# Adding transfers for the square sums, plain products three tiles behind, and the token scale spread inside the third plain tile

## The chip, the cores and the metric

The kernel runs on one core of a Trainium2 chip. Its time is the device time of one execution in microseconds (us); of several runs the median counts. The engines are TensorE (PE, matmuls), VectorE (DVE), ScalarE (ACT), GpSimd (POOL) and SyncE (SP, which here issues the DMA transfers).

## The reference, cut to what matters

The model is a trunk of two layers over 1024 frames of width 1024. Layer 0 mixes with stick-breaking attention and a pooling branch, layer 1 with gated linear attention. After the mixer each layer adds a feed-forward part with a depthwise convolution, and its input is normalised:

```python
def rms_norm(x, gain):
    xf = x.astype(jnp.float32)
    y = xf * lax.rsqrt(jnp.mean(xf * xf, axis=-1, keepdims=True) + NORM_EPS)
    return (y * gain.astype(jnp.float32)).astype(x.dtype)
...
def conv_ffn(h, w_up, conv_w, conv_b, w_down):
    u = h @ w_up
...
    a, g = jnp.split(conv, 2, axis=-1)
    return (jax.nn.silu(a) * g) @ w_down
...
x = x + conv_ffn(rms_norm(x, ffn_norm[layer]), ffn_w_up[layer], ...)
```

The case is about the entry into `h @ w_up`: the end of the mixer's output projection, the sum of squares of x over its 1024 channels, and the first columns of the up-projection.

## The kernel before, in words

The activations lie transposed: eight tiles x[0] to x[7] of 128 channels (partitions) by 1024 frames, in float32. A product in near-float32 precision is made of three matmuls in a faster format (`mm3`, lines 137, 139, 141): each operand is split into a high and a low part, and high x high, high x low and low x high are summed in PSUM. PSUM has eight banks of 128 x 512; in this stage the tags lin, z, t and d name two banks each, taken in turn (`bank`).

`ffn` is called once in each layer. Its entry, which this text calls entry A in layer 0 and entry B in layer 1, goes like this. `add_tiles` (from line 809) makes the last two row blocks of the mixer's output projection for one tile of x, 12 matmuls, first for frames 0 to 511 into a bank of t, then for frames 512 to 1023 into a bank of d; after each half DVE adds the bank to x (line 819). `NormBlocks.add` (line 293) then spills x to memory through SP (line 295), makes the tile's two blocks (line 289 on ACT the high part, line 290 on DVE the low part, with the gain already in), squares x on ACT (lines 306, 309) and adds the square to the accumulator nacc on DVE (line 310). Tiles come in the order 0, 4, 1, 5, 2, 6, 3, 7 (`ORDER`). Two tiles behind, `first_tile` (line 976) lets the tile enter two ordinary ("plain") products of the up-projection, 12 matmuls: column tile 0 into the banks lin with the weights s12h and s12l, and its gate into the banks z with s34h and s34l.

After the eight tiles `stats` (line 258) sums nacc over partitions by matmuls with ones (line 261), takes the root on ACT (264) and the reciprocal on DVE (266), and puts it on a diagonal dg (line 268; the tile is called ndg in A and nsq in B). `plain(1)` makes a third plain column tile, 48 matmuls in eight steps of six, into banks of t and d. Then `spread` (line 273) multiplies dg by ones into a bank of d and one of t (line 275), which gives the reciprocal root for each frame on all partitions, and ACT copies it to rstd_bc (276). DVE multiplies the three finished column tiles by rstd_bc to u (line 1008), and `plain(FT + 1)`, the fourth plain tile, takes the banks lin and z again. From then on the up-projection goes by pairs in a Strassen-like scheme (`Pair`, matmuls on line 885), whose operands `rsums` and `rblock` (lines 905 to 908 and 864, 865) prepare from x during the entry. The pair's first evacuations are tm on ACT (926, 933, 941) and u on DVE (937, 942, 948, 952).

Three things set the order of the work. PE runs in the order in which the code is written. The instructions of DVE, ACT, POOL and SP are ordered by the framework's scheduler when the kernel is built, and each engine then works through its queue in that order and waits at its head. Large buffers come from pools: x, nacc, the squares, T4 and u share eleven slots of 128 x 1024 (`slot`), the blocks share sixteen (`hpool`), and a new tile waits for the old one in its slot.

Of the kernel before, what the change touches and what calls it, by code (L numbers as in the profile page):

```python
# [13 lines left out]
AF = mybir.ActivationFunctionType  # L14
ALU = mybir.AluOpType
# [4 lines left out]
KT = D // P  # L20
# [36 lines left out]
def trunk_kernel(  # L57
# [23 lines left out]
    V, S, G, PE = nc.vector, nc.scalar, nc.gpsimd, nc.tensor  # L81
# [21 lines left out]
    def bank(tag):  # L103
        return psum.tile([P, 512], F32, tag=f"bank{next(turns[tag])}", name=tag)
# [4 lines left out]
    ORDER = [0, 4, 1, 5, 2, 6, 3, 7]  # L109


    def load_split(src, pool=None, tags=("whi", "wlo", "wraw"), eng=None, nb=2, raw=None, parts=None):
        n = src.shape[1]
        pool = pool or wpool
        if raw is None:
            raw = (pool if len(tags) > 2 else wpool).tile([P, n], F32, tag=tags[2] if len(tags) > 2 else "wraw",
                                                      name="wraw", bufs=2 if "draw" in tags else 1)
        hi = pool.tile([P, n], R32, tag=tags[0], name="whi", bufs=nb)
        lo = pool.tile([P, n], R32, tag=tags[1], name="wlo", bufs=nb)

        def part(cs):
            nc.sync.dma_start(raw[:, cs], src[:, cs])
            S.copy(hi[:, cs], raw[:, cs])  # L123
            (eng or V).tensor_tensor(lo[:, cs], raw[:, cs], hi[:, cs].bitcast(F32), op=ALU.subtract)  # L124

        if parts is not None:
            parts.extend(lambda cs=cs: part(cs) for cs in HALVES)
        else:
            part(slice(0, n))
        return hi, lo  # L130

    def mm3(out, w, a, first, last):

        (wh, wl), (ah, al) = w, a
        n = len(out)
        for i in range(n):
            PE.matmul(out[i], wh, ah[i], start=first, stop=False)  # L137
        for i in range(n):
            PE.matmul(out[i], wh, al[i], start=False, stop=False)  # L139
        for i in range(n):  # L140
            PE.matmul(out[i], wl, ah[i], start=False, stop=last)  # L141
# [11 lines left out]
    class Filler:  # L153
# [3 lines left out]
        def add(self, *gens):  # L157
            self.gens += gens
# [119 lines left out]
    class NormBlocks(Norm):  # L278
# [14 lines left out]
        def add(self, m, x):  # L293
            xs[m] = dram.tile([P, T], F32, tag=f"xs{self.layer}_{m}", name="xs")
            nc.sync.dma_start(xs[m], x)
            g = pcol(self.col + m)
            if m < KT // 2:
                self.b11.append(self.block(x[:, 0:512], g))
                self.b12.append(self.block(x[:, 512:T], g))
            else:  # L300
                self.b21.append(self.block(x[:, 0:512], g))
                self.b22.append(self.block(x[:, 512:T], g))
            self.n += 1
            if self.n == 1:
                self.acc = self.acc_tile()
                S.activation(self.acc, x, AF.Square)
            else:
                sq = self.sq_tile()
                S.activation(sq, x, AF.Square)
                V.tensor_tensor(self.acc, self.acc, sq, op=ALU.add)  # L310
            if m < KT // 2:
                S.activation(x, x, AF.Copy, scale=g)

# [22 lines left out]
    def pcol(c):  # L336
        return prm[:, c:c + 1]
# [244 lines left out]
    x = [None] * KT  # L582
# [227 lines left out]
    def add_tiles(ws, acts, tags, ms):  # L810
        n = len(ws)
        pss = {m: [bank(next(tags)), bank(next(tags))] for m in ms}
        for i, cs in enumerate(HALVES):
            for m in ms:
                sl = slice(m * P, (m + 1) * P)
                for k in range(n):
                    mm3([pss[m][i]], (ws[k][0][:, sl], ws[k][1][:, sl]),
                        ([acts[k][0][:, cs]], [acts[k][1][:, cs]]), k == 0, k == n - 1)
                V.tensor_tensor(x[m][:, cs], x[m][:, cs], pss[m][i], op=ALU.add)  # L819
# [7 lines left out]
    def ffn(layer, nm, after, ow, mixt, onward=None):  # L827
# [10 lines left out]
        def raw_a(i):  # L838
            raw = wpool.tile([P, T], F32, tag="wraw", name="wraw", bufs=1)
            nc.sync.dma_start(raw, wup[layer, i])  # L840
            hi = wpool.tile([P, T], R32, tag="whi", name="whi")
            lo = wpool.tile([P, T], R32, tag="wlo", name="wlo")
            S.copy(hi, raw)
            V.tensor_sub(lo, raw, hi.bitcast(F32))
            return raw, hi, lo
# [30 lines left out]
        tags = itertools.cycle(("lin", "z", "t", "d"))  # L876
# [14 lines left out]
        def rblock(n, k):  # L891
            if n == "T4" and k < 3:
                t = slot(R32, "T4")
            elif n == "T1":
                t = hpool.tile([P, T], R32, tag="h", name="blk")
            else:
                t = ut(f"{n}_{k}")
            src = {"T1": x[k][:, T0], "T3": x[k][:, T1], "T2": x[k + 4][:, T1], "T4": x[k + 4][:, T0]}[n]
            split(t[:, T0], t[:, T1], src)
            rhs[n][k] = t  # L900
# [59 lines left out]
                                   op0=ALU.mult, op1=ALU.add)  # L960


        first = []
        for i, hl, raw, tag in ((0, (s12h, s12l), s12, "lin"), (FT, (s34h, s34l), s34, "z")):
            nc.sync.dma_start(raw, wup[layer, i])
# [3 lines left out]
        def plain_tile(w, ps, n):  # L969
            k = ORDER[n]  # L970
            rt = (nm.b11[k], nm.b12[k]) if k < 4 else (nm.b21[k - 4], nm.b22[k - 4])
            sl = slice(k * P, (k + 1) * P)
            mm3(ps, (w[0][:, sl], w[1][:, sl]), ([t[:, T0] for t in rt], [t[:, T1] for t in rt]),
                n == 0, n == KT - 1)

        def first_tile(n):
            for w, ps in first:
                plain_tile(w, ps, n)

        def plain(i, tags):  # L980
            w, ps = raw_a(i)[1:], [bank(t) for t in tags]
            for n in range(KT):
                plain_tile(w, ps, n)
            return ps

        otags = itertools.cycle("td")
        add_tiles(ow, mixt, otags, ORDER[:2])
        for n, m in enumerate(ORDER):
            if n >= 2:
                add_tiles(ow, mixt, otags, [m])  # L990
            nm.add(m, x[m])
            if n >= 2:
                first_tile(n - 2)
        for k in range(4):
            rsums(k)
            for n in ("T4", "T2", "T3"):
                rblock(n, k)
        first_tile(KT - 2)
        first_tile(KT - 1)
        nm.stats("t")  # L1000
        ps = plain(1, "td")
        nm.spread(iter("dt"))
        us = []

        def evacuate(ps):
# [4 lines left out]
        for b in [b for _, b in first] + [ps]:  # L1010
            evacuate(b)
        ps = plain(FT + 1, ("lin", "z"))
        for k in range(4):
            rblock("T1", k)
# [74 lines left out]
        tags = itertools.cycle(("lin", "z", "t", "d"))  # L1089
# [42 lines left out]

    norm.sq_tile = lambda: slot(F32, "nsq")
    ffn(0, n0, lambda m: norm.add(x[m]), ws, [mix[k] for k in last], onward)


    ev = ExitStack()
    op = ev.enter_context(tc.tile_pool(name="odd", bufs=1, reuse_waits="tile"))
# [231 lines left out]
    for hd in range(GH):  # L1370
# [3 lines left out]
        if hd < GH - 1:  # L1374
# [3 lines left out]
            mixt = next(g)  # L1378
# [6 lines left out]
        else:  # L1385
# [4 lines left out]
            mixt = next(g)  # L1390
            next(g)
            run(r, g)
            ow = [load_split(woo[2 * hd]), load_split(woo[2 * hd + 1])]
    ev.close()

    nnorm = NormBlocks(1, C_FFN1, lambda: slot(F32, "nacc"), lambda: slot(F32, "nsq"))
    ffn(1, nnorm, lambda m: [nc.sync.dma_start(yT[m * P:(m + 1) * P, cs], x[m][:, cs]) for cs in HALVES],
        ow, mixt)

# [63 lines left out]
```

## Time and profile before

| | us |
|---|---|
| median of 3 runs | 2277.08 |
| lowest, highest | 2275.28, 2280.37 |
| the profiled execution | 2277.86 |
| its span, first to last instruction | 2275.8 |
| entry A, first added tile to the end of the fourth plain tile | about 422 to 496 |
| entry B, the same | about 1559 to 1637 |

The profile is of one execution. A row of the timeline gives start and duration in us from the span's start, engine, line, what is written from what, and how many instructions are merged; in brackets stands how long the engine sat idle before and what released it. Matmuls are pipelined, so the start of the next one tells more than the duration. The granted clock is the share of full speed that PE got.

### The profile page before, as it was taken

The numbers are of one execution on the slowest core, as the hardware profiler recorded it, in microseconds if no ns is written. First come the engines' busy times: TensorE is split into PE (matmuls) and PEld (weight loads), VectorE is DVE, ScalarE is ACT, GpSimd is POOL, SyncE is SP. The second block draws the span as 40 slices with busy tenths as digits, with TensorE's granted clock in tenths as the row PEclk, the third lists the DMA queues.
The fourth block names the chain that finished last, engine by engine and source line by source line (L and its number), as shares of the span: only waits on it lengthen the run. The fifth ranks groups of instructions, "written<-read, shape, count | busy, mean of one in ns | idle before, by whom it ended". The sixth has DMA issues, their size and how long they took to land.

```text
span 2275.8 us, 27397 instructions
## 1 busy us (share of the span) xinstructions
PE 2217.9 (97%) x10648; PEld 1827.0 (80%) x10648; DVE 1643.6 (72%) x2238; ACT 1010.0 (44%) x1533; POOL 318.5 (14%) x197
## 2 busy tenths in 40 slices
PE   8999989999999999999999999999999999999999
PEld 7889878877888887888887878787778888878887
DVE  5687688799999998554546455548899999985543
ACT  6666665454444444221246252527544444442210
POOL 2230120001111113321200000000011111133210
PEclk9999999999999999999999999999999999999999
DMA  4132441222222226331011011112222222264211
GB/s 143 62 99 80 113 138 52 103 74 84 79 80 83 84 84 234 137 111 47 0 48 38 28 47 38 45 31 102 75 74 84 83 84 84 84 220 141 102 47 74
DMA packets 56898, 194.26 MB, mean 85 GB/s; under 512 B 6832, under 2 KB 7472, under 8 KB 56768
## 3 DMA queue, kind: packets, MB, share of 16 engines
q1 hardware_dynamic: 56768, 192.51, 25.6%
q8 instruction: 84, 1.38, 0.2%
q14 instruction: 46, 0.38, 0.1%
HBM read 149.49 MB, written 42.99 MB: 85 GB/s over the span
## 4 chain that ended last, share of the span: by engine, by line
PE 83%; DVE 6%; ACT 4%; issue 4%; DMA 2%; POOL 1%; SPq 0%; DVEq 0%; ACTq 0%; POOLq 0%
PE lin L885 13%; PE z L885 9%; PE lin L137 5%; PE lin L139 5%; PE lin L141 5%; PE t L885 4%; PE d L885 4%; PE z L137 3%; PE z L139 3%; PE z L141 3%; PE t L137 3%; PE t L139 3%; PE t L141 3%; PE d L139 2%; PE d L137 2%
## 5 line engine op out<-in xcount | busy, mean ns | idle before, releaser
L123 ACT CAST whi<-wraw 128x1024 fp32r<-128x1024 f32 (+4 forms) x108 | 107.7, 999 | 367.6 <-PE d L139 231.8
L1077 POOL TENSOR_TENSOR c<-c 128x1024 f32<-128x1024 f32 x44 | 109.3, 2483 | 900.9 <-ACT c L1076 884.9
L124 DVE TENSOR_TENSOR wlo<-wraw,whi 128x1024 fp32r<-128x1024 f32 (+3 forms) x94 | 137.4, 1461 | 34.4 <-ACT whi L123 33.7
L911 DVE TENSOR_TENSOR u<-u,rstd_bc 128x512 f32<-128x512 f32 x160 | 159.7, 999 | 2.6
L956 ACT ACTIVATE c<-u,prm 128x1024 f32<-128x1024 f32 x88 | 109.6, 1245 | 76.8 <-DVE u L911 69.4
L1106 POOL TENSOR_TENSOR act<-a,act 128x1024 fp32r<-128x1024 f32 x40 | 105.7, 2650 | 219.7 <-ACT act L1105 217.9
L137 PE MATMUL lin<-h_hi,whi 128*128 128x512 f32 x304 | 119.9, 433 | 6.8 <-ACT whi L123 5.9
L819 DVE TENSOR_TENSOR x<-x,t 128x512 f32<-128x512 f32 x105 | 71.8, 684 | 66.5 <-PE t L141 66.3
L959 DVE SCALAR_TENSOR_TENSOR c<-u,prm,c 128x1022 f32<-128x1022 f32 x88 | 118.7, 1349 | 0.1
L957 DVE SCALAR_TENSOR_TENSOR c<-u,prm,c 128x1023 f32<-128x1023 f32 x88 | 112.5, 1278 | 6.5 <-ACT c L956 6.4
L675 DVE TENSOR_TENSOR_SCAN pt<-pt,z 128x128 f32<-128x128 f32 (+3 forms) x96 | 93.1, 970 | 33.2 <-ACT z L668 32.2
L885 PE MATMUL d<-T,a 128*128 128x512 f32 x480 | 115.3, 389 | 0.0
L819 DVE TENSOR_TENSOR x<-x,d 128x512 f32<-128x512 f32 x105 | 71.8, 684 | 57.6 <-PE d L141 57.6
L139 PE MATMUL lin<-h_lo,whi 128*128 128x512 f32 x304 | 110.2, 401 | 1.1 <-DVE h_lo L247 1.1
L141 PE MATMUL lin<-h_hi,wlo 128*128 128x512 f32 x304 | 110.1, 401 | 0.0
L885 PE MATMUL z<-blk,s34h 128*128 128x512 f32 x320 | 100.7, 396 | 6.0 <-DVE u L942 6.0
L885 PEld LDWEIGHTS d<-T,a 128*128 128x128 f32 x480 | 90.1, 188 | 18.7
L864 ACT CAST s12h<-s 128x1024 fp32r<-128x1024 f32 x42 | 44.2, 1052 | 135.2 <-PE lin L885 123.9
L885 PE MATMUL lin<-T,s34h 128*128 128x512 f32 x320 | 98.9, 390 | 1.9 <-ACT tm L933 1.9
L885 PE MATMUL z<-blk,s12h 128*128 128x512 f32 x320 | 100.7, 396 | 0.0
L885 PE MATMUL lin<-blk,whi 128*128 128x512 f32 x320 | 99.8, 393 | 0.0
L885 PE MATMUL lin<-T,s12h 128*128 128x512 f32 x320 | 99.5, 392 | 0.0
(428 smaller groups left out, 6350.3 us busy)
## 6 DMA issues: line engine op xcount, KB each, us to landing
wraw<-in_wup SPq DMA_DIRECT2D x44, 512.0 KB, 3.6
act<-c SPq DMA_DIRECT2D x44, 512.0 KB, 2.6
wraw<-in_wdn SPq DMA_DIRECT2D x44, 512.0 KB, 3.6
raw_g<-in_wup SPq DMA_DIRECT2D x40, 512.0 KB, 3.5
a<-act SPq DMA_DIRECT2D x40, 512.0 KB, 4.3
xs<-x SPq DMA_DIRECT2D x16, 512.0 KB, 2.6
x<-xs SPq DMA_DIRECT2D x16, 512.0 KB, 6.0
x<-in_xT SPq DMA_DIRECT2D x8, 512.0 KB, 5.8
```

Of the source, the lines that this page charges most:

```text
L123: S.copy(hi[:, cs], raw[:, cs])
L124: (eng or V).tensor_tensor(lo[:, cs], raw[:, cs], hi[:, cs].bitcast(F32), op=ALU.subtract)
L137: PE.matmul(out[i], wh, ah[i], start=first, stop=False)
L139: PE.matmul(out[i], wh, al[i], start=False, stop=False)
L141: PE.matmul(out[i], wl, ah[i], start=False, stop=last)
L819: V.tensor_tensor(x[m][:, cs], x[m][:, cs], pss[m][i], op=ALU.add)
L885: PE.matmul(ps, w, m, start=first and k == 0 and n == 0, stop=k == 3 and n == 2, skip_group_check=True)
L911: V.tensor_tensor(dst, dst, rstd_bc[:, cs], op=ALU.mult)
L956: S.activation(c, u, AF.Identity, scale=pcol(b + 2), bias=pcol(b + 3))
L957: V.scalar_tensor_tensor(c[:, 1:], u[:, :T - 1], pcol(b + 1), c[:, 1:], op0=ALU.mult, op1=ALU.add)
L959: V.scalar_tensor_tensor(c[:, 2:], u[:, :T - 2], pcol(b), c[:, 2:], op0=ALU.mult, op1=ALU.add)
L1077: G.tensor_tensor(ca, ca, cg, op=ALU.mult)
```

## The change

It has three parts, all in the entry.

Five square sums by adding transfers: the first square becomes `part`, the squares of tiles 2 to 6 in the order are added to `part` by transfers that POOL issues and that add in the destination, the seventh square becomes `acc`, and after the eighth DVE makes two additions, acc + square and acc + part.

Plain products three tiles behind: `AHEAD = 3`. Three tiles of the output projection are now made together at the start (halves of frames 0 to 511 of all three, then of 512 to 1023), and `first_tile` runs three tiles behind the additions.

Spread amid the third plain tile: `plain` takes a function to be called after its fifth step of eight, and the call for the third plain tile gives it `nm.spread`.

```diff
             self.n += 1
+            sq = self.acc_tile() if self.n == 1 else self.sq_tile()
+            S.activation(sq, x, AF.Square)
             if self.n == 1:
-                self.acc = self.acc_tile()
-                S.activation(self.acc, x, AF.Square)
+                self.part = sq
+            elif self.n < KT - 1:
+                G.dma_start(self.part, sq, accum_op=ALU.add)
+            elif self.n == KT - 1:
+                self.acc = sq
             else:
-                sq = self.sq_tile()
-                S.activation(sq, x, AF.Square)
                 V.tensor_tensor(self.acc, self.acc, sq, op=ALU.add)
+                V.tensor_tensor(self.acc, self.acc, self.part, op=ALU.add)
...
+        AHEAD = 3
...
-        def plain(i, tags):
+        def plain(i, tags, amid=None):
             w, ps = raw_a(i)[1:], [bank(t) for t in tags]
             for n in range(KT):
                 plain_tile(w, ps, n)
+                if n == 4 and amid is not None:
+                    amid()
             return ps
...
-        add_tiles(ow, mixt, otags, ORDER[:2])
+        add_tiles(ow, mixt, otags, ORDER[:AHEAD])
         for n, m in enumerate(ORDER):
-            if n >= 2:
+            if n >= AHEAD:
                 add_tiles(ow, mixt, otags, [m])
             nm.add(m, x[m])
-            if n >= 2:
-                first_tile(n - 2)
+            if n >= AHEAD:
+                first_tile(n - AHEAD)
...
-        first_tile(KT - 2)
-        first_tile(KT - 1)
+        for n in range(KT - AHEAD, KT):
+            first_tile(n)
         nm.stats("t")
-        ps = plain(1, "td")
-        nm.spread(iter("dt"))
+        ps = plain(1, "td", lambda: nm.spread(iter("dt")))
```

DVE's queue at the start of entry B, before (x_7591, x_7599 and x_7593 are the first three tiles of x in the order; t and d the banks that are added):

```order
L819 TENSOR_TENSOR x_7599<-x_7599,t_12867 128x512
L865 TENSOR_TENSOR s12l_12851<-s12_12848,s12h_12850 128x1024
L290 SCALAR_TENSOR_TENSOR blk_12899<-x_7591,prm_77,blk_12899 128x512
L819 TENSOR_TENSOR x_7591<-x_7591,d_12866 128x512
L865 TENSOR_TENSOR s34l_12853<-s34_12849,s34h_12852 128x1024
L856 TENSOR_TENSOR s12_12848<-raw_g_12847 128x512
L865 TENSOR_TENSOR a22_12854<-raw_g_12847,a22_12854 128x512
L819 TENSOR_TENSOR x_7599<-x_7599,d_12868 128x512
L819 TENSOR_TENSOR x_7593<-x_7593,t_12919 128x512
```

The same place now:

```order
L824 TENSOR_TENSOR x_7599<-x_7599,t_12867 128x512
L870 TENSOR_TENSOR s12l_12851<-s12_12848,s12h_12850 128x1024
L290 SCALAR_TENSOR_TENSOR blk_12915<-x_7591,prm_77,blk_12915 128x512
L824 TENSOR_TENSOR x_7593<-x_7593,t_12869 128x512
L870 TENSOR_TENSOR s34l_12853<-s34_12849,s34h_12852 128x1024
L861 TENSOR_TENSOR s12_12848<-raw_g_12847 128x512
L870 TENSOR_TENSOR a22_12854<-raw_g_12847,a22_12854 128x512
L824 TENSOR_TENSOR x_7591<-x_7591,d_12866 128x512
L824 TENSOR_TENSOR x_7599<-x_7599,d_12868 128x512
L290 SCALAR_TENSOR_TENSOR blk_12918<-x_7591,prm_77,blk_12918 128x512
L824 TENSOR_TENSOR x_7593<-x_7593,d_12870 128x512
```

The third tile's first half (t_12869) is added where the first tile's second half (d_12866) stood, and d_12866 comes four places later, behind s34l, s12 and a22. The bank of d_12870 is that of d_12866.

ACT's queue in entry A, before, from the second square on (x_4153, x_3717, x_4254 and x_3830 are tiles 2 to 5 of the order; the names in brackets are the semaphores waited for, DMASW those of POOL's transfers):

```order
L309 ACTIVATE ndg_4553<-x_4153 128x1024
L289 ACTIVATE blk_4574<-x_3717,prm_77 128x512 [waits DVE_49]
L312 ACTIVATE x_3457<-x_3457,prm_77 128x1024 [waits DMAHW2_49,DVE_49,Activation_49]
L289 ACTIVATE blk_4577<-x_3717,prm_77 128x512 [waits DVE_49]
L309 ACTIVATE ndg_4580<-x_3717 128x1024
L312 ACTIVATE x_3717<-x_3717,prm_77 128x1024 [waits DMAHW4_49,DVE_49,Activation_49]
L289 ACTIVATE blk_4614<-x_4254,prm_77 128x512 [waits DVE_49]
L864 CAST T3_0_4803<-x_3457 128x512 [waits DVE_49,PE_49]
L289 ACTIVATE blk_4617<-x_4254,prm_77 128x512 [waits DVE_49]
L309 ACTIVATE ndg_4620<-x_4254 128x1024
```

The same place now:

```order
L306 ACTIVATE ndg_4580<-x_3717 128x1024
L289 ACTIVATE blk_4602<-x_4254,prm_77 128x512 [waits DVE_49]
L289 ACTIVATE blk_4605<-x_4254,prm_77 128x512 [waits DVE_49]
L306 ACTIVATE ndg_4608<-x_4254 128x1024 [waits DMASW0_49,Activation_49]
L317 ACTIVATE x_3717<-x_3717,prm_77 128x1024 [waits DMAHW4_49,DVE_49,Activation_49]
L869 CAST T3_0_4791<-x_3457 128x512 [waits DVE_49,PE_49]
L289 ACTIVATE blk_4641<-x_3830,prm_77 128x512 [waits DVE_49]
L869 CAST T2_0_4788<-x_4153 128x512 [waits DVE_49]
L289 ACTIVATE blk_4644<-x_3830,prm_77 128x512 [waits DVE_49]
L306 ACTIVATE ndg_4647<-x_3830 128x1024 [waits DMASW1_49]
```

The fourth square waits for the first adding transfer, the fifth for the second, and so on to the eighth, which waits for the fifth; the blocks of the next tile stand behind each of them.

POOL's queue in entry A is now (it held nothing there before):

```order
L310 DMA nacc_4558<-ndg_4569 128x1024 [waits PE_49,Activation_49]
L310 DMA nacc_4558<-ndg_4580 128x1024 [waits DMASW0_49,Activation_49]
L310 DMA nacc_4558<-ndg_4608 128x1024 [waits DMASW1_49,Activation_49]
L310 DMA nacc_4558<-ndg_4647 128x1024 [waits DMASW2_49,Activation_49]
L310 DMA nacc_4558<-ndg_4687 128x1024 [waits DMASW3_49,Activation_49]
```

Each transfer waits for the one before it and for its square.

## The prediction

> **What bounds the kernel now.** Read first: the page. TensorE (PE) is busy for 97% of the span, so only time in which it waits, or runs slowly, is to be had. The profiled execution took 2277.86 us (span 2275.8, 2.06 around it), 0.78 above the median 2277.08 of the runs; differences worked out in the trace are taken off the median.
>
> ```profile
> PE 2217.9 (97%) x10648; PEld 1827.0 (80%) x10648; DVE 1643.6 (72%) x2238; ACT 1010.0 (44%) x1533; POOL 318.5 (14%) x197
> ```
>
> Read second: busy time in two stretches, the tiles of entry A (layer 0) and entry B (layer 1) up to the statistics. Columns: stretch, length, busy time and count of PE, weight loads, VectorE (DVE), ACT, POOL, then granted clock and DMA. DVE works 38.47 of 38.60 us in A and 41.19 of 42.00 in B, more than PE: it is what PE waits for here.
>
> ```profile
> 430.20:468.80 38.60, 36.60 (x157) 29.17 (x156) 38.47 (x56) 26.09 (x35) 0.00 (x0) 1.00 0.28 110
> 1570.00:1612.00 42.00, 39.43 (x171) 31.98 (x172) 41.19 (x58) 27.67 (x38) 0.00 (x0) 0.96 0.30 112
> ```
>
> Read third: PE's timeline at the waits (start, duration; in brackets the idle time by the profile).
>
> ```profile
> 430.65 0.40 PE L139 MATMUL lin<-blk,s12h 128*128 128x512 f32 x1
> 432.27 0.50 PE L139 MATMUL lin<-blk,s12h 128*128 128x512 f32 x1 [1.22 <-DVE blk L290]
> 432.60 0.64 PE L141 MATMUL lin<-blk,s12l 128*128 128x512 f32 x2
> 433.07 0.62 PE L137 MATMUL z<-blk,s34h 128*128 128x512 f32 x2
> ...
> 462.65 0.40 PE L139 MATMUL lin<-blk,s12h 128*128 128x512 f32 x1
> 463.83 0.50 PE L139 MATMUL lin<-blk,s12h 128*128 128x512 f32 x1 [0.78 <-DVE blk L290]
> 464.17 0.62 PE L141 MATMUL lin<-blk,s12l 128*128 128x512 f32 x2
> ...
> 468.81 1.84 PE L261 MATMUL t<-ones,nacc 128*128 128x2 f32 x16
> ...
> 481.50 1.02 PE L275 MATMUL d<-ndg,ones 128*128 128x512 f32 x2
> 482.35 1.02 PE L275 MATMUL t<-ndg,ones 128*128 128x512 f32 x2
> 484.19 0.50 PE L137 MATMUL lin<-blk,whi 128*128 128x512 f32 x1 [0.82 <-DVE u L1008]
> 484.79 0.50 PE L137 MATMUL z<-blk,whi 128*128 128x512 f32 x1
> ```
>
> Matmuls follow each other every 0.23 us (432.60 to 433.07 is two). So in A the first plain tile loses 432.27 - 430.65 - 0.23 = 1.39, and 0.10 at the next start: 1.49. The seventh loses 0.95 + 0.11 = 1.06. The spread (2 x 0.85 of work) should end at 483.20; the next product starts at 484.19, 0.99 late, and its second bank, 0.60 behind it in place of 0.23, loses 0.37: 1.36, a wait for u, which waits for rstd_bc.
>
> ```profile
> 1601.12 0.40 PE L139 MATMUL lin<-blk,s12h 128*128 128x512 f32 x1
> 1603.37 0.50 PE L139 MATMUL lin<-blk,s12h 128*128 128x512 f32 x1 [1.85 <-DVE blk L290]
> 1603.71 0.66 PE L141 MATMUL lin<-blk,s12l 128*128 128x512 f32 x2
> 1604.17 1.05 PE L137 MATMUL z<-blk,s34h 128*128 128x512 f32 x2
> ...
> 1607.58 0.63 PE L139 MATMUL lin<-blk,s12h 128*128 128x512 f32 x2
> ...
> 1609.90 1.84 PE L261 MATMUL t<-ones,nacc 128*128 128x2 f32 x16
> 1605.00:1606.00 1.00, 1.00 (x4) 0.78 (x3) 1.00 (x3) 0.00 (x0) 0.00 (x0) 0.50 0.44 176
> ```
>
> In B the seventh tile loses 2.02 + 0.11 = 2.13, and then eight matmuls take 3.41 us in place of 1.86: the granted clock in that stretch (last row, third figure from the end) is 0.50. That costs 1.55 more.
>
> ```profile
> 1568.73 0.40 PE L139 MATMUL lin<-blk,s12h 128*128 128x512 f32 x1
> 1570.72 0.50 PE L139 MATMUL lin<-blk,s12h 128*128 128x512 f32 x1 [1.59 <-DVE blk L290]
> 1623.48 1.02 PE L275 MATMUL t<-nsq,ones 128*128 128x512 f32 x2
> 1625.32 0.50 PE L137 MATMUL lin<-blk,whi 128*128 128x512 f32 x1 [0.82 <-DVE u L1008]
> ```
>
> B's first tile loses 1.76 + 0.10 = 1.86, and no slow clock follows; its spread loses 1625.32 - 1624.33 = 0.99 and, as in A, 0.37: 1.36. To be had: A 1.49 + 1.06 + 1.36 = 3.91, B 1.86 + 2.13 + 1.55 + 1.36 = 6.90.
>
> **The change, part by part.**
>
> *Products three tiles behind.* The first plain tile starts one added tile later (2.73 us, 12 x 0.227) than its block needs, and the seventh two plain tiles (5.6 us) after the last added tile in place of one. With no more than the old DVE work ahead of the blocks, all of 1.49 + 1.06 and 1.86 + 2.13 + 1.55 goes. What is late next: the third added tile now stands among the first three, and its two halves use the banks of the first tile, so its second half waits until DVE has added the first tile's second half to x. In A that addition now stands behind s34l:
>
> ```profile
> 427.93 1.22 DVE L865 TENSOR_TENSOR s34l<-s,s34h 128x1024 fp32r<-128x1024 f32 x1
> 429.06 0.68 DVE L819 TENSOR_TENSOR x<-x,d 128x512 f32<-128x512 f32 x1
> ...
> 1562.78 0.39 PE L137 MATMUL d<-mh,whi 128*128 128x512 f32 x1
> 1568.12 0.69 DVE L865 TENSOR_TENSOR a<-raw_g,a 128x512 fp32r<-128x512 f32 x1
> 1568.72 0.68 DVE L819 TENSOR_TENSOR x<-x,d 128x512 f32<-128x512 f32 x1
> ```
>
> The queue ahead of it is as long as before, so it runs at 429.06 and ends at 429.74; PE would be there at 428.83 (the first product's second step at 430.65, less two matmuls and a half tile of 1.36): a new wait of 0.9 and the late start's 0.1, 1.0. In B it moves behind s34l, s and a, to the slot of 1568.72, and ends at 1569.40; PE is there at 1562.78 + 3 x 1.36 = 1566.86: a new wait of 2.6. Both start from DVE's own times before, which this part does not shift. Of the waits above 1.59 was not followed by the slow clock and 1.85 was; 2.6 is nearer to 1.85, so 1.55 is added in B, none in A. New cost: A 1.0, B 4.15. The Trainium skill, "TensorE: Matmul & The Clock Gate" (Why this matters for your kernels), warns only of idle gaps over about 3 us; by it B would pay no 1.55 and the forecast would be 1.55 lower. The row with 1.85 speaks against the page, so the row decides.
>
> *Adding transfers.* Seven DVE additions in each entry (1.13 from one start to the next, as at 427.93 for that size) become two: 5.65 us of DVE time leave a queue that had no gap. That is what lets the blocks keep up; it is not a gain of its own. In their place come five transfers on POOL, which did nothing in either stretch. They add into one tile, so each waits for the one before, and a Square on ACT waits for the transfer two before it (it reuses the buffer), the last Square for the fifth. Behind these Squares ACT holds the blocks that PE's plain tiles need. No such transfer is in the trace. L, its time from issue to landing, is bounded by a plain store below and by the slowest transfer of 512 KB in the rows of x and xs above:
>
> ```profile
> act<-c SPq DMA_DIRECT2D x44, 512.0 KB, 2.6
> x<-xs SPq DMA_DIRECT2D x16, 512.0 KB, 6.0
> ...
> DMA to landing us min/median/max: 2.6/3.0/8.6
> ...
> GB/s 0 0 0 233 255 408 36 135 331 0 7 0 0 0 317 149 0 0 0 0 277 189 0 149 324 0 15 0 164 302 0 0 233 233 58 284 124 0 0 0
> L289 ACT ACTIVATE blk<-x,prm 128x512 fp32r<-128x512 f32 x16 | 11.1, 717 | 13.8 <-DVE x L819 12.5 <-PE d L139 1.3
> L309 ACT ACTIVATE ndg<-x 128x1024 f32<-128x1024 f32 x7 | 7.3, 1046 | 2.9 <-DVE x L819 2.9
> ```
>
> At 408 GB/s 512 KB take 1.3 us; an adding transfer reads a second tile, so 2.6 + 1.3 = 3.9, and something for POOL's issue and for the spills of x beside it: I take 4.9. The Trainium skill, "DMA: Bandwidth & Descriptors" (Anatomy of one DMA), prices a GpSimd transfer at 2.0 us plus its bytes at 436 GB/s; with the second read that is an estimate of 4.4, by which the sum below is the same. When is it late? After the first tile's second half is in x, at 429.74, ACT does three blocks of 0.72 and two Squares of 1.05 (4.25) before the first transfer leaves, at 434.0 in A. The statistics start at 468.81 - 2.55 + 1.0 = 467.3. Before them stand the last Square (1.05) and on DVE two additions of 1.22 with a half-width step of 0.60 between (3.0): the fifth transfer must have landed by 463.3. So five L fit in 29.3: L up to 5.9. In B it is 1569.40 + 4.25 = 1573.65 and 1609.90 - 5.54 + 4.15 - 4.05 = 1604.5: L up to 6.2. Below that the adds cost nothing; beyond, PE waits 5 us for each us of L in each entry.
>
> *Spread amid the third tile.* The scale's diagonal, dg, was ready 4.8 us after the statistics (475.44, and 468.81 + 1.84):
>
> ```profile
> 474.22 1.22 DVE L268 TENSOR_TENSOR ndg<-ident,rstd_tok 128x1024 f32<-128x1024 f32 x1
> ```
>
> In A DVE's queue between the two is now as long as before, to a step. The fifth step of the third tile ends 30 x 0.227 = 6.8 us after the statistics, 2 us later than dg. The remaining 18 matmuls (4.1 us) cover the copies of rstd_bc on ACT and the first u on DVE. The spread's own 1.7 us stay. Gain 1.36 in each entry; if the cover failed it would be the old wait again.
>
> *After the entry* PE waits twice in the first pair of each layer:
>
> ```profile
> 507.80 0.73 PE L885 MATMUL lin<-T,s34h 128*128 128x512 f32 x2 [1.04 <-ACT tm L933]
> 514.85 0.73 PE L885 MATMUL z<-blk,s34h 128*128 128x512 f32 x2 [1.31 <-DVE u L942]
> ```
>
> ACT's c now stands behind the copy of tm, and DVE comes to the pair with more lead; against that, other steps now stand ahead of u. Between -2.35 and +2.35 in each layer; I take a gain of 0.4 in each.
>
> Sum: A 3.91 - 1.0 = 2.9, B 6.90 - 4.15 = 2.75, pairs 0.8: 6.45 us. 2277.08 - 6.45 = 2270.6.
>
> **Rivals.** (1) *The chain of transfers is late.* For it: five in a row with a wait each, beside 512 KB spills on the same DMA engines, on an issue path the trace does not show; the loads of x from xs, issued in company, took 6.0. Against: 4.9 leaves 1 us each. The cost is 10 x L - 60.5; it eats the gain at L = 6.7 and is 0.2% from L = 7.2. At 7.5 it is 14.5: 2277.08 - 6.45 + 14.5 = 2285.1, slower; at 8.6 it is 25.5: 2296.1. (2) *The waits only move.* The new wait for the bank lasts over 1.8 in A too and takes the clock with it (2.4 more), and the pairs lose 2.4 in place of gaining 0.8: 6.45 - 2.4 - 3.2 = 0.85, 2276.2, no change. For it: DVE's order at the third tile is the worst for PE; against: DVE has 5.65 us less to do. (3) *More goes:* no slow clock in B and all of the pairs' waits away: 6.45 + 1.55 + 3.9 = 11.9, 2265.2. The Trainium skill's clock page, as cited above, gives the first part of it.
>
> **Chances.** A measurement of this kernel tells about 0.2% (4.6 us) from no change. Forecast 0.58, nearly all of it beyond 4.6 us; (1) 0.21, of which 0.05 within 4.6 us; (2) 0.16, of which 0.01 slower; (3) 0.05. With 0.06 of the forecast falling short: faster 0.57, same 0.26, slower 0.17. Range: 2265 (rival 3) to 2284 (rival 1 at L = 7.4).
>
> **What would show it.** Right: the waits of lin L139 for blk gone, 1.0 and 2.6 before the third tile's second half, the slow clock moved to it in B; no wait between L275 and lin L137; L310 at 4 to 6 us each, no PE wait before L261. Wrong: ACT's Squares waiting for a DMA past 463 in A, L261 late, or a DVE gap before its last addition.

## The result, and the profile after

The changed kernel takes 2284.23 us (median of 7 runs, 2280.53 to 2286.42), the kernel before in the same comparison 2275.63 (7 runs, 2271.42 to 2280.37). The ratio is 1.003, with a 95% interval of 1.0019 to 1.0042: slower, by 6.8 us by the ratio and 8.6 by the two medians, where 6.5 less was forecast. The profiled execution of the changed kernel took 2280.53 (span 2278.4), the lowest of its 7.

Its page shows in two lines that the place of the limit has moved. First the busy times, then the chain of work that ended last, by engine:

```profile
PE 2220.5 (97%) x10648; PEld 1824.4 (80%) x10648; DVE 1624.2 (71%) x2228; ACT 999.7 (44%) x1533; POOL 330.9 (15%) x207
...
PE 76%; DVE 10%; ACT 5%; DMA 4%; issue 4%; POOL 0%; SPq 0%; ACTq 0%; DVEq 0%; POOLq 0%
```

The same line of the kernel before:

```profile
PE 83%; DVE 6%; ACT 4%; issue 4%; DMA 2%; POOL 1%; SPq 0%; DVEq 0%; ACTq 0%; POOLq 0%
```

DVE has 19 us less to do and yet 10% of the chain in place of 6%, and DMA has 4% in place of 2%: PE is now led by DVE and by transfers for longer. Where? PE runs the same matmuls in both kernels, so the start of one and the same matmul in both traces says how far the changed kernel is ahead (minus) or behind (plus) at that point:

| matmul (us from the span's start) | before | after | after less before |
|---|---|---|---|
| entry A, first added tile | 422.01 | 419.76 | -2.25 |
| layer 0, second pair, first of z (s34h) | 534.93 | 528.88 | -6.05 |
| layer 0, first of the down-projection | 886.76 | 885.68 | -1.08 |
| entry B, first added tile | 1558.95 | 1558.19 | -0.76 |
| layer 1, second pair, first of z (s34h) | 1675.16 | 1670.28 | -4.88 |
| layer 1, first of the down-projection | 2026.89 | 2029.10 | +2.21 |

So the entries, with the first pair behind them, won 3.81 and 4.12 us (forecast 3.3 and 3.15). That this is so close is in part luck: up to the first pair's z (514.85, now 506.98, and 1655.81, now 1650.58) 5.62 and 4.47 were won, and 1.8 and 0.35 of it were lost again up to the second pair's. The pairs after them, which the forecast took as unchanged, lost 4.97 and 7.09, and from there to the end only 0.4 more is lost. (The 2.25 ahead of entry A and the 0.3 between the layers lie in code that is the same; the last section shows what can make such shifts.)

The entries as forecast: PE's timeline of the changed kernel at the new wait for the bank in A, at the statistics and the spread, and at the same new wait in B:

```profile
427.55 0.50 PE L137 MATMUL d<-whi 128*128 128x512 f32 x1 [0.83 <-DVE x L824]
...
465.14 1.84 PE L261 MATMUL t<-ones,ndg 128*128 128x2 f32 x16
...
473.80 1.02 PE L275 MATMUL d<-ndg,ones 128*128 128x512 f32 x2
474.65 1.02 PE L275 MATMUL t<-ndg,ones 128*128 128x512 f32 x2
475.11 0.79 PE L137 MATMUL t<-blk,whi 128*128 128x512 f32 x1
...
1568.70 0.50 PE L137 MATMUL d<-mh,whi 128*128 128x512 f32 x1 [2.17 <-DVE x L824]
1569.84 0.63 PE L139 MATMUL d<-ml,whi 128*128 128x512 f32 x1
1570.27 0.63 PE L141 MATMUL d<-mh,wlo 128*128 128x512 f32 x1
```

The waits of lin for blk are gone, the statistics stand 3.67 earlier than at 468.81 (2.25 of it from ahead of the entry, 1.42 from the entry itself; 1.29 in B; forecast 1.55 and 1.39), the spread runs without a wait around it, and in B the slow clock follows the new wait (matmuls 0.43 apart from 1569.84 on). The five transfers, on POOL's timeline in A (idle time in brackets), then the time from issue to landing (median of A and of B; least, median and most of all ten):

```profile
431.70 1.04 POOL L310 DMA_DIRECT2D nacc<-ndg  x1 [92.76 <-ACT ndg L306]
...
452.42 0.85 POOL L310 DMA_DIRECT2D nacc<-ndg  x1 [4.24 <-DMA nacc<-ndg]
```

```profile
nacc<-ndg POOLq DMA_DIRECT2D x5, 512.0 KB, 4.7
nacc<-nsq POOLq DMA_DIRECT2D x5, 512.0 KB, 4.5
```

```profile
DMA to landing us min/median/max: 4.5/4.6/5.8
```

From one issue to the next they take (452.42 - 431.70) / 4 = 5.18 us, below the 5.9 that was free. Nothing waits for them on PE.

The pairs: what each engine waited for between 500 and 2030 us (total, times, longest), first in the kernel before, then in the changed one:

```profile
ACT whi L843 <- DMA wraw<-in_wup: 46.0, 35, 1.8
PEld z L885 <- DVE u L942: 8.1, 5, 1.8
PE z L885 <- DVE u L942: 6.0, 5, 1.4
DVE wlo L844 <- ACT whi L843: 2.2, 1, 2.2
```

```profile
ACT whi L848 <- DMA wraw<-in_wup: 97.8, 34, 4.1
DVE wlo L849 <- ACT whi L848: 31.4, 34, 2.1
PEld z L890 <- DVE u L947: 25.5, 40, 1.9
PE z L890 <- DVE u L947: 10.2, 11, 1.4
```

DVE's wlo waits for whi 34 times, in nearly every pair, in place of once, and PE's weight loads for z wait for u 40 times in place of 5. A middle pair shows why. DVE before and after, from the second half of s34 (line 861, now 866) to the addition that reads the bank z (line 942, now 947):

```profile
719.40 0.69 DVE L861 TENSOR_TENSOR s<-wraw,s 128x512 f32<-128x512 f32 x1
720.00 1.28 DVE L959 SCALAR_TENSOR_TENSOR c<-u,prm,c 128x1022 f32<-128x1022 f32 x1
...
725.39 1.21 DVE L844 TENSOR_TENSOR wlo<-wraw,whi 128x1024 fp32r<-128x1024 f32 x1
726.53 0.67 DVE L942 TENSOR_TENSOR u<-tm,z 128x512 f32<-128x512 f32 x1
```

```profile
717.18 1.28 DVE L964 SCALAR_TENSOR_TENSOR c<-u,prm,c 128x1022 f32<-128x1022 f32 x1
718.37 0.69 DVE L866 TENSOR_TENSOR s<-wraw,s 128x512 f32<-128x512 f32 x1
...
723.82 1.23 DVE L849 TENSOR_TENSOR wlo<-wraw,whi 128x1024 fp32r<-128x1024 f32 x1 [0.81 <-ACT whi L848]
724.96 0.68 DVE L947 TENSOR_TENSOR u<-tm,z 128x512 f32<-128x512 f32 x1
```

The second half of s34 is the last reader of the raw weight tile, which has one buffer. Before, it stood ahead of the pair's last convolution step (line 959, now 964); now it stands behind it, 1.19 us later (1.41 when both are counted from PE's z at 708.67 and at 706.23). SP's load of the next raw tile waits for it, ACT makes whi from the load, DVE makes wlo from whi, and the addition that frees the bank z stands behind wlo. The other engines' rows for the same pair, before:

```profile
708.67 0.62 PE L885 MATMUL z<-blk,s34h 128*128 128x512 f32 x2
...
720.11 0.33 SPq L840 DMA_DIRECT2D wraw<-in_wup  x1
...
723.80 1.05 ACT L843 CAST whi<-wraw 128x1024 fp32r<-128x1024 f32 x1 [1.36 <-DMA wraw<-in_wup]
...
727.96 0.62 PE L885 MATMUL z<-blk,s34h 128*128 128x512 f32 x2
```

and after:

```profile
706.23 0.72 PE L890 MATMUL z<-blk,s34h 128*128 128x512 f32 x2
...
719.09 0.33 SPq L845 DMA_DIRECT2D wraw<-in_wup  x1
...
722.74 1.05 ACT L848 CAST whi<-wraw 128x1024 fp32r<-128x1024 f32 x1 [2.78 <-DMA wraw<-in_wup]
...
725.70 0.72 PE L890 MATMUL z<-blk,s34h 128*128 128x512 f32 x2
```

From the load's issue to PE's z there were 727.96 - 720.11 = 7.85 us before; now there are 725.70 - 719.09 = 6.61, and the chain takes all of it: load 3.6, whi 1.05, wlo 1.2, the addition 0.7. The spare time was 0.54 ahead of wlo (whi done at 724.85, wlo from 725.39) and 0.76 behind the addition (727.20 to 727.96), 1.30 in all. The convolution step eats 1.19 of it, which with the hand-overs on the way leaves none. From this pair to the next PE now takes 19.47 us in place of 19.29, and whatever makes a load late goes straight into PE's time: in layer 1 the load that SP issues at 1877.83 brings its wlo only at 1883.47, 5.64 later in place of 4.73, and PE waits.

```profile
1885.35 0.73 PE L890 MATMUL z<-blk,s34h 128*128 128x512 f32 x2 [0.81 <-DVE u L947]
```

The scheduler put the last step of the convolution ahead of s34's second half in 17 pairs of each layer, though no line of the pairs was edited. A few other neighbours changed places with it (an earlier convolution step and a scaling of u, another one and the second half of s12, and on ACT a convolution step and a copy of tm). All of them stand ahead of s34's second half in both orders, so they move neither it nor what follows it; that is argued from their places and was not tested alone.

### The profile page after: what moved, and what is told of

Read it like the earlier page. It is cut to its first block, busy times and chain, and to the rows that moved or that the text cites. A ratio compares the mean times of both kernels' runs of the same rounds, so it can differ in the third digit from the quotient of the medians.

```text
span 2278.4 us, 27410 instructions
## 1 busy us (share of the span) xinstructions
PE 2220.5 (97%) x10648; PEld 1824.4 (80%) x10648; DVE 1624.2 (71%) x2228; ACT 999.7 (44%) x1533; POOL 330.9 (15%) x207
## 4 chain that ended last, share of the span: by engine, by line
PE 76%; DVE 10%; ACT 5%; DMA 4%; issue 4%; POOL 0%; SPq 0%; ACTq 0%; DVEq 0%; POOLq 0%
PE lin L890 10%; PE z L890 8%; PE lin L137 5%; PE lin L139 5%; PE lin L141 5%; PE t L890 3%; PE d L890 3%; PE z L141 3%; PE z L137 3%; PE z L139 3%; PE t L137 3%; PE t L139 3%; PE t L141 3%; PE d L137 3%; PE d L141 3%
## 5 line engine op out<-in xcount | busy, mean ns | idle before, releaser
L890 PE MATMUL t<-blk,whi 128*128 128x512 f32 x320 | 98.7, 390 | 0.0
```

What stands on the lines that cost most here:

```text
L890: PE.matmul(ps, w, m, start=first and k == 0 and n == 0, stop=k == 3 and n == 2, skip_group_check=True)
```

## The experiments

Theory 1: this order in the pairs is the loss, and the entries do what was forecast. Theory 2: the order is harmless, and the software queue's transfers or the new entries cost the time. Ratios stand against the kernel before on the same chip; its median was 2275.43 us (29 runs) for the first four kernels, 2275.87 (29) for the next four and 2274.98 (30) for the last four.

**The order alone (e1, e2).** In e1 the kernel before gets the new order in its pairs: sum34 leaves its second half out, and that half comes behind the last convolution step (`issue_after` ties what stands in its block behind an instruction in the queue of that engine; nothing more is waited for):

```diff
-                sum34(i + 2)
+                sum34(i + 2, True)
...
-            conv(i, ua, ca)
+            last = conv(i, ua, ca)
+            if 0 < i < FT - 2:
+                with tc.issue_after(last.ins):
+                    V.tensor_tensor(s34[:, T1], raws[i + 2][:, T1], s12[:, T1], op=ALU.subtract)
```

> The kernel before with one instruction tied: from the third pair on, the second half of s34 (its last read of the raw tile) stands behind the last convolution operation of its pair on DVE, as the scheduler has it in the changed kernel; the entries are the old ones. Theory 1 (the pairs' new order on DVE is the loss: it frees the raw tile later, the next load, whi and wlo come later, and the bank z behind wlo): PE's pair grows from 19.29 us to about 19.5 in both layers, 17 pairs each, so 2 x 17 x 0.21 = 7 us slower, 2281 to 2285 against 2275.6. Theory 2 (the order is harmless; the transfers of the software queue or the entries themselves cost it): 2274 to 2277, no wait at z in the pairs.

In e2 the changed kernel gets the old order back:

```diff
-            V.scalar_tensor_tensor(c[:, 2:], u[:, :T - 2], pcol(b), c[:, 2:],
-                                   op0=ALU.mult, op1=ALU.add)
+            with tc.issue_after(behind.ins) if behind is not None else nullcontext():
+                V.scalar_tensor_tensor(c[:, 2:], u[:, :T - 2], pcol(b), c[:, 2:],
+                                       op0=ALU.mult, op1=ALU.add)
...
-                sum34(i + 2)
+                s4 = sum34(i + 2)
...
-            conv(i, ua, ca)
+            conv(i, ua, ca, s4)
```

> The changed kernel with the last convolution operation of each pair tied behind the second half of s34 on DVE: the pairs stand as before from the third on, the entries are the new ones. Theory 1: what the pairs lost between the two traces goes (3.85 us in layer 0, 5.56 in layer 1), the pair is at 19.29 us again and the entries' gain stays: 6 to 8 us under the kernel before, 2267.5 to 2270. Theory 2: 2281 to 2285, as the changed kernel.

e1 took 2292.89 us, ratio 1.0072 (1.005 to 1.0094): 17.5 us slower by the medians with not a line of its entries touched, more than twice what was expected. In its trace the pairs lost 5.91 us in layer 0 and 7.73 in layer 1: beside the steady 0.2 per pair, single waits of up to 1.5 us at z. e2 took 2266.58, ratio 0.9957 (0.9939 to 0.9974), just below what was expected: one instruction tied turns the loss into a gain of 9 to 10 us. Waits between 500 and 2030 us in e1, and then in e2, where DVE's wlo waits for whi once in place of 35 times:

```profile
DVE wlo L844 <- ACT whi L843: 33.9, 35, 2.4
PE z L886 <- DVE u L943: 12.4, 10, 1.5
```

```profile
PE z L890 <- DVE u L947: 3.7, 4, 1.4
DVE wlo L849 <- ACT whi L848: 0.6, 1, 0.6
```

The signature comes and goes with the tie of one instruction. (The scheduler turns the few other places over along with it: e1's pairs stand in the whole order of the changed kernel, e2's in that of the kernel before. The two runs test the order, not the one step.) Theory 2 falls.

**What stands ahead of z (e3).** e3 is the changed kernel with the late order tied as in e1, and with wlo tied behind the addition that reads z:

```diff
-                V.tensor_tensor(self.ug[:, T1], self.u3, self.B, op=ALU.add)
+                self.z7 = V.tensor_tensor(self.ug[:, T1], self.u3, self.B, op=ALU.add)
...
+                if i > 2 and nx:
+                    with tc.issue_after(p.z7.ins):
+                        V.tensor_sub(A[i + 1][1], raws[i + 1], A[i + 1][0].bitcast(F32))
```

> The changed kernel with the new order tied (second half of s34 behind the last convolution operation), and wlo of the next pair tied behind the addition that reads the bank z, where it stood ahead of it. Theory 1: the raw tile is still freed late and whi still comes late, but nothing that waits for it stands ahead of z on DVE, so PE no longer waits there: the pair at 19.29 us, 5 to 8 us under the kernel before, 2268 to 2271. Rival to its last link (DVE itself is too late for z in this order, whatever stands there): pairs of 19.4 to 19.5 us and 2278 to 2285.

2272.39 us, ratio 0.9982 (0.9969 to 0.9995): a miss by 1.4 us, and 5.8 above e2. By the trace the pairs are at 19.29, nothing is lost in them, and the entries win 4.87 in A, as in e2, and 5.18 in B, of which 1.55 is the slow clock that e2's trace has there and e3's has not. The trace reaches entry A 6.0 us later than e2's does, in code that is the same, which is more than the 4.5 us between the two spans (2268.3 and 2263.8); whether that holds for the other runs of e3 is not shown. DVE and SP in e3 (s34's second half is line 1090 there, wlo line 1070):

```profile
718.60 1.27 DVE L966 SCALAR_TENSOR_TENSOR c<-u,prm,c 128x1022 f32<-128x1022 f32 x1
719.79 0.68 DVE L1090 TENSOR_TENSOR s<-wraw,s 128x512 f32<-128x512 f32 x1
...
724.50 0.69 DVE L949 TENSOR_TENSOR u<-tm,z 128x512 f32<-128x512 f32 x1
725.10 1.22 DVE L1070 TENSOR_TENSOR wlo<-wraw,whi 128x1024 fp32r<-128x1024 f32 x1
```

```profile
707.09 0.33 SPq L845 DMA_DIRECT2D wraw<-in_wup  x1
726.38 0.33 SPq L845 DMA_DIRECT2D wraw<-in_wup  x1
```

The rival (DVE itself too late in this order) falls: with the late order kept, PE does not wait. But the expectation was wrong in one more point. The load does not come late any more: it is now freed by wlo (725.10 to 726.32, load at 726.38) and no longer by the sums, so e3 takes the whole chain from s34 over the load to z apart and not only its last link. It shows that the chain is the cause, not which link of it would have been enough.

**The spread's place (e5, e9).** e5 is the kernel before with the spread amid the third plain tile and nothing else (`plain(1, "td", lambda: nm.spread(iter("dt")))`); e9 is the same with the tie of e2.

> The kernel before with the spread amid the third plain tile alone, nothing tied. Its pairs stand in the new order on DVE by themselves (second half of s34 behind the last convolution operation). Theory 1 now reads: the spread's place alone turns the pairs' order over, and that costs what the new order cost with the old entry (17.5 us by the medians), less the spread's own gain of 2 x 1.36: 2286 to 2292, pairs of 19.5 us and more. Rival (it takes all three parts; the entry's other waits put the pairs into the order that hurts): 2272 to 2276 with pairs of 19.29 us.

> The spread amid alone on the kernel before, with the pairs tied in the old order. The same edit untied gave 2286.2. Theory 1: the pairs are at 19.29 us from the second on, and the spread's gain shows. By the forecast it is 2 x 1.36, and about 1.6 us go in the first pair: 2273 to 2275. If the spread also takes away the waits of the first pair that stood in the trace of before (u for lin 0.8, tm for lin 1.0, u for z 1.3), it is 2.3 to 4 us per layer: 2269 to 2272. Theory 2 (the pairs' order has nothing to do with the spread's loss): 2284 and more.

e5 took 2286.16 us, ratio 1.0043 (1.0025 to 1.0062); e9 2269.72, ratio 0.9968 (0.9957 to 0.998). Busy time and matmuls (the x behind PE's figure) in 200 us of the pairs, e5 and then e9:

```profile
600.00:800.00 200.00, 199.00 (x861) 160.78 (x860) 182.13 (x206) 85.22 (x101) 24.45 (x10) 1.00 0.25 79
```

```profile
600.00:800.00 200.00, 200.00 (x873) 163.68 (x872) 184.45 (x208) 91.87 (x105) 26.45 (x11) 1.00 0.26 84
```

The spread's place alone turns the order over, and PE's records hold 12 matmuls less in these 200 us at the same granted clock. By what reckoning the scheduler turns the order is not shown here. Tied, it is worth more than the 1.36 of the forecast: e9's entries win 2.30 in A, and 5.06 in B, of which 1.55 is the slow clock that B happens not to have there. The order's price in three settings is nearly the same: e1 0.72%, e5 less e9 0.75%, the changed kernel less e2 0.73%, each about 16.5 us.

**The other parts (e4, e6, e7, e10, e11).** These kernels leave one part of the change out or take one alone; the pairs are in the old order in all of them, by the scheduler's own choice (e4, e6, e11) or by the tie of e2 (e7, e10).

```diff
-        AHEAD = 3
+        AHEAD = 2
...
-        ps = plain(1, "td", lambda: nm.spread(iter("dt")))
+        ps = plain(1, "td")
+        nm.spread(iter("dt"))
```

e4 has both of these edits to the changed kernel, e6 the second, e10 the first; e7 and e11 have the square sums of the kernel before in place of the transfers, e11 with the second edit as well.

> The kernel before with the adding transfers alone; two tiles ahead and the spread at its old place. The pairs keep the old order on DVE. Theory 1: the pairs cost nothing, 5.65 us of DVE time per entry are free, of which at most the wait for blk (1.49 and 1.86 us by the prediction) is won: 2272 to 2276. Theory 2 (the software queue's transfers cost the time): 2280 to 2285.

> The changed kernel without the spread amid: the adding transfers and three tiles ahead, the spread at its old place, nothing tied; the pairs keep the old order on DVE. Theory 1: the pairs are at 19.29 us, the waits of lin for blk in the entries are gone, the spread's 2 x 1.36 are not won: 8.9 less 2.7, so 6 us under the kernel before, 2268 to 2271. Rival (three tiles ahead only moves the waits to the third added tile's bank, 0.8 and 2.2 us, and the spread gave nearly the whole gain of the tied kernel): 2273 to 2276.

> The changed kernel with the pairs tied in the old order, and the five square sums back on DVE in place of the transfers. If the transfers carry part of the tied kernel's gain (5.65 us of DVE time in each entry that blk and u would wait for): 2270 to 2274, with waits of PE for blk or x on DVE in both entries. If three tiles ahead has already made DVE's time in the entries free: 2265 to 2268, as the tied kernel with transfers (2266.6).

> The changed kernel with the pairs tied in the old order and two tiles ahead in place of three. If three ahead carries what the forecast gives it (1.49 + 1.06 less 1.0 in layer 0, 1.86 + 2.13 + 1.55 less 4.15 in layer 1, so 2.9): 2268.5 to 2271 beside the tied kernel's 2266.6, with waits of lin for blk back in both entries. If it only moves waits: 2265 to 2268.

> The kernel before with three tiles ahead alone, adds on DVE, spread at its old place; the pairs keep the old order on DVE. By the forecast's terms 2.9 us less: 2271 to 2274. If the freed time is given back before the first pair, where the plain tiles' evacuations wait for the spread, as transfers with three ahead did (2275.9): 2275 to 2277.

Times by the runs; the entries by the traces, from the first added tile to the second pair's z as in the first table, less the same in the kernel before:

| kernel | us | ratio (95%) | entry A | entry B |
|---|---|---|---|---|
| e4 transfers alone | 2275.60 | 1.0001 (0.9984 to 1.0018) | -1.12 | -1.35 |
| e11 three ahead alone | 2271.69 | 0.9982 (0.997 to 0.9995) | -0.63 | -1.03 |
| e9 spread amid alone, tied | 2269.72 | 0.9968 (0.9957 to 0.998) | -2.30 | -5.06 |
| e6 without the spread amid | 2275.88 | 1.0003 (0.999 to 1.0015) | -2.57 | -0.93 |
| e10 without three ahead, tied | 2267.49 | 0.9964 (0.9949 to 0.998) | -4.01 | -5.58 |
| e7 without transfers, tied | 2270.20 | 0.9975 (0.9961 to 0.9988) | -3.76 | -3.22 |
| e2 all three, tied | 2266.58 | 0.9957 (0.9939 to 0.9974) | -4.76 | -4.85 |

In entry B, 1.55 of the figures of e4, e9 and e10 is again the slow clock that is missing in their traces. What follows: the transfers alone neither cost time, as theory 2 had it, nor gave any. e6 is a miss: 2268 to 2271 was expected of it, and it shows nothing by the runs, though its trace wins in both entries; it lies in the range of the rival, by which three ahead only moves the waits. e10 is as fast as e2 within the intervals, so three ahead is worth little beside the other two; alone (e11) it gave 3.3 us by the medians, but only 1.7 of that lies in its entries. e7's two entries are 1.0 and 1.6 behind e2's, so the transfers do carry something there; by the runs that is within the intervals. With intervals of some 3 us to either side the runs don't price the parts one by one.

**Both ties (e8, e12).** e8 is e2 with the second tie of e3; e12 leaves that one off for the wlo of the last pair.

> The changed kernel with both ties: second half of s34 ahead of the last convolution operation, and wlo behind the addition that reads z. With the first tie alone the first pair of layer 0 took 20.90 us in place of 19.29, with the late order and the second tie 19.36. If that wait is of wlo ahead of z, too, the two together win another 1.5 us in layer 0: 2263 to 2266. If it is of the convolution operation that the scheduler put ahead of z in the first pair, nothing more is won: 2265 to 2268.

> Both ties as in the run before that had them, with the second one (wlo behind the addition that reads z) left off in the last two pairs, where that run took 21.62 us in place of 20.85 in each layer. If those are won: 1.5 us under it, 2263 to 2265. If not: 2265 to 2266.5.

e8 took 2265.61, ratio 0.9957 (0.9942 to 0.9971), the same as e2, and a time that both of its expectations allow: the first pair of layer 0 is at 19.29 and its entries win 6.37 and 6.97 (in B again 1.55 of it by the slow clock that is missing), but the pairs behind give 0.66 and 1.12 back (the last one takes 21.62 in place of 20.85). e12 took 2271.06, ratio 0.9977 (0.9963 to 0.999), a miss: its pairs lost 5.29 us in layer 0 and 2.71 in layer 1, with PE waiting for u at z again, up to 2.0 and 2.2 us at once. In layer 0, 1.66 of the loss is a piece of slow clock that follows such a wait. The longest one stands where the last pair's wlo, now untied, runs at 846.60 ahead of the sums, and DVE works without a gap from 843.66 to the addition that PE waits for (857.26); what makes the shorter waits is open. The fastest kernels are e2 and e8, some 10 us below the kernel before and 17 below the changed one.

## Why the prediction was wrong, step by step

**What is to be had, and three tiles ahead:** right. All waits of lin for blk went. The waits that took their place were forecast as 1.0 and 2.6 and are 0.83 (and the start's 0.1) and 2.17, with the slow clock behind the second.

**The adding transfers:** right. L was taken as 4.9; it is 4.7 in A and 4.5 in B. The estimate from the Trainium skill's "DMA: Bandwidth & Descriptors" (Anatomy of one DMA), its fit with the second read added, was 4.4: the trace agrees to 0.3 us. Rival 1, which held nearly all of the chance for slower, did not happen: the sign came out on its side for another reason.

**The spread:** too low. The forecast gave it 1.36 per entry; by e9 it is 2.30 in A. Besides the wait of the fourth plain tile for u it takes away the first pair's wait of lin for tm (1.04) and shortens that of z for u, from 1.31 to 0.5; up to there 3.6 is won, and 1.3 is lost again in the second pair, where lin now waits 1.04 for tm. In B e9's trace has 5.06. Of it 1.55 is the clock and 1.06 a shorter wait of the seventh tile for blk (0.77 in place of 1.85), both ahead of the spread; the spread's own part is 4.1 up to the first pair's z, less 1.6 in the second pair, where z waits 1.52 for u: 2.45.

**After the entry:** this is the step that failed. It reads that PE waits twice in the first pair of each layer and bounds the effect of the new order at 2.35 us per layer. The new order does not end with the first pair. It runs through 17 more in each layer, which the forecast took as unchanged; PE was busy there without a wait. Their 19.29 us was the longer of two cycles: PE's own work, and the chain from the raw tile's last reader to the bank z, which had 1.30 us to spare. Moving one step of 1.19 us ahead of that last reader cost 4.97 + 7.09 = 12.1 us in the profiled execution. The order's whole price is more, since it begins in the pairs that the table counts with the entries: from the first added tile to the down-projection the changed kernel's trace is 5.9 and 7.8 us behind e2's, 13.7 together, and e5's behind e9's the same. By the runs it is 16.5; the difference lies within their intervals of some 4 us to either side. The forecast's 0.8 for the pairs, its only term for them, stands against this. Rival 2 had the right place, waits that move into the pairs, but its loss of 2.4 in both layers together was that of a first pair.

**The slow clock in B:** the forecast won 1.55 and paid it again, so the sum did not feel it, but the reason given (1.85 is followed by it, 1.59 is not) does not hold: a wait's length alone does not decide. e1 has the old entry with the same wait, and no slow clock; PE's timeline, then the stretch behind it (granted clock third from the end):

```profile
1612.37 0.50 PE L139 MATMUL lin<-blk,s12h 128*128 128x512 f32 x1 [1.85 <-DVE blk L290]
```

```profile
1611.50:1617.00 5.50, 4.63 (x20) 3.79 (x21) 5.50 (x9) 3.78 (x6) 0.00 (x0) 1.00 0.29 95
```

## What to carry to other kernels

Where a scheduler orders the queues, an edit in one place can turn over the order of a loop far behind it: set the whole program's order before against the order after, and give a difference in a steady loop its weight times the loop's count. A loop that looks bound by one engine has other cycles beside it, of a buffer's last reader, the load that waits for it and what stands ahead of the next hand-over; their spare time, read from one turn in the trace, says how far any of their steps may move. When a gain that shows in the trace at its place is not in the time, look for where the lead is lost again: the same instruction's start in both traces finds it, and one tied instruction tests it.

## What the runs showed of the hardware

An adding transfer of 512 KB in float32 from SBUF to SBUF, issued by POOL, took 4.5 to 5.8 us to land, median 4.6, and held POOL for 0.85 to 1.04; a chain of five, each waiting for the one before, ran at 5.18 us each beside the loads and spills of the entry.

The granted clock falls to 0.50 in pieces of some 3.4 us, and their places differ between traces where the code is the same. The stretch from 100 to 200 us in the kernel before, then in the changed one:

```profile
100.00:200.00 100.00, 96.56 (x578) 83.29 (x577) 79.37 (x148) 68.50 (x150) 23.75 (x26) 0.98 0.38 115
```

```profile
100.00:200.00 100.00, 96.40 (x586) 82.93 (x585) 79.91 (x149) 69.50 (x152) 23.80 (x26) 1.00 0.40 116
```

A wait of 2.17 was followed by it in the changed kernel and one of 2.15 in e3 was not, as its timeline and the stretch around it show:

```profile
1566.70 0.50 PE L137 MATMUL d<-mh,whi 128*128 128x512 f32 x1 [2.15 <-DVE x L824]
```

```profile
1565.00:1572.00 7.00, 5.30 (x23) 4.38 (x24) 6.44 (x11) 5.32 (x8) 0.89 (x1) 1.00 0.57 226
```

The Trainium skill's page "TensorE: Matmul & The Clock Gate" (Why this matters for your kernels) warns of gaps over about 3 us; here waits of about 2 us were followed by the slow clock in some runs and not in others. In each trace the pieces begin whole steps of 3.41 us from one another (in the kernel before at 184.2, 269.6 and 1604.2, the last two 25 and 416 steps behind the first), and this grid lies elsewhere in each trace. The wait of 2.17 lies within one such step (1566.2 to 1569.6), the one of 2.15 in e3 across two (one ends at 1566.0); but e1's wait of 1.85 lies within one too, but for 0.03 us, so this alone does not decide it either. Such a piece cost 1.55 us in entry B. Pieces in different places shift the traces against each other in code that is the same: between 269.97 and 272.96 of the kernel before, which has a piece there, the changed kernel, which has none, gets 1.4 us ahead. That is part of the 2.25 us ahead of entry A, and an effect of one or two us is not to be read from a pair of single traces without looking at the clock in each stretch.
